# Window attention in a diffusion backbone: score products of full height, and the mask added where the row maximum is taken

## The chip, the cores and the metric

The kernel runs as one program on one core of a Trainium2 chip. The metric is the device time of one execution in microseconds (us), the median of several runs. The engines of the core work side by side, each through its own queue in order: TensorE (PE, with its weight loads shown apart as PEld), VectorE (DVE), ScalarE (ACT), GpSimd (POOL) and SyncE (SP), which issues most of the DMAs. Matrix products are summed in PSUM, and all other tiles lie in SBUF.

## What is computed

The reference is a stack of two layers over 256 latent tokens and 256 context tokens of width 1024. Each layer is a half-step SwiGLU FFN, a token mixer, and another half-step FFN; the mixer of layer 0 is a gated DeltaNet, that of layer 1 windowed attention with a sink per head. Only layer 1's mixer matters here, and only its latent queries, since the last layer's context output is not used:

```
s_ctx = einsum('bqhgd,bkhd->bhgqk', qb, kc)                 # 256 context keys, no mask
s_win = where(allowed, einsum('bqhgd,bkhd->bhgqk', qb, kb), -inf)   # |t - s| <= 128
p = _sink_softmax(concatenate([s_ctx, s_win]), sink)
o = einsum(p[..., :ctx_len], vc) + einsum(p[..., ctx_len:], vb)
```

There are 16 query heads of 64 features and 4 key heads; four query heads share one key head. With 256 latent tokens in two blocks of 128 queries, the window of a block covers all 256 latent keys, so every query sees 512 keys, and only one 128 by 128 corner of the latent keys is partly masked for each block.

## The kernel before

All products are made in a fast form of fp32 (`F32R`) that keeps the high part of a number alone. So each operand is split into a high part and a low part (number minus high part), and a product is made as high by high, high by low, and low by high, summed in PSUM. A weight matrix is loaded into a tile, split by ScalarE (high part) and by VectorE or GpSimd (low part) into working tiles, and then used.

The working tiles `u` are 76 buffers of 128 by 512 fp32 (256 KB each), and PSUM has 8 banks `mm`. The program is straight-line: the class `Sched` keeps an estimated clock of TensorE work and of each engine, and decides by it in which order the instructions are emitted. Background generators (`yield` gives the time at which they wish to be resumed) are woven between the products of the main line. On the chip nothing is reordered: each engine runs its instructions in the emitted order and waits for what they need.

The attention goes so:

- `att_consts` is started in the last part of the FFN ahead of it. It loads the constants over SP, among them the two triangles of the mask, and ScalarE copies these into `wmask`, 128 by 384: a triangle for either block with a zero square between, so that a slice of 256 columns is the mask of block 0 or block 1.
- `attention` makes keys and values first (four units of 128 columns for all 512 tokens), then the queries in 8 units of two heads, latent tokens only.
- `att_qk` norms and rotates a unit of two heads (64 rows each). For keys it writes the high part of each head twice, into rows 0 to 63 and 64 to 127 of a tile `st[par]`, and the low parts of both heads into one tile `lo`, each in its own 64 rows. For queries `st[par]` holds the high part in the head's own 64 rows and the low part in the other 64.
- Four `att_worker` generators take the 16 pairs of a query unit and a block. For each of the two heads of a pair (`par`), TensorE makes a score tile of 128 queries by 512 keys in three products: the query tile, 128 rows, with the doubled high keys (which gives high by high and low by high at once); the identity with the mask, 256 latent columns; and the high query, 64 rows, with the low keys, 64 rows. That is 32 score tiles in all. VectorE then takes the row maximum of each, ScalarE the exponential with the negative maximum as its bias and the row sum as a second output, VectorE scales by the reciprocal, TensorE transposes the probabilities, ScalarE copies them out, and TensorE multiplies them with the values.
- When few pairs are left, the output product begins (`begin`), and `out_blocks` finishes it and starts the next norm.

The score products and the maximum, as they stand (lines 1751 to 1760):

```
for par in range(2):
    rw = slice(64 * par, 64 * par + 64)
    sc.append(self.cht())
    self.mm(sc[par], q[par][:, qs], kh[par], stop=False)
    self.mm(sc[par][:, LAT], self.identr, self.wmask[:, 128 - 128 * qt:384 - 128 * qt], start=False, stop=False)
    self.mm(sc[par], q[par][rw, qs], kl[rw, :], start=False)
...
for par in range(2):
    nc.vector.tensor_reduce(out=st[:, 0, par:par + 1], in_=sc[par], axis=AX.X, op=ALU.max)
```

In the profile most instructions of VectorE, ScalarE, GpSimd and SP carry line 180, that of the helper that records them, products carry line 276 and transposes line 281, so groups are told apart by their tiles.

Of the kernel before, what the change touches and what calls it, by code (L numbers as in the profile page):

```python
# [6 lines left out]
F32R = mybir.dt.float32r  # L7
AF = mybir.ActivationFunctionType
ALU = mybir.AluOpType
# [13 lines left out]
def constants():  # L23
    """Arrays that depend on shapes alone."""
    c = {"ident": np.eye(128, dtype=np.float32)}
    # 128 rows: two chunks of 64 tokens; in variant e the half e runs forward and the other one backward
# [20 lines left out]
    d = np.arange(64)  # L47
# [13 lines left out]
    c["atc"] = at  # L61
    return c


class Sched:
    """Emission order: straight-line code advances a clock of TensorE work, and
    background generators are resumed when the clock reaches the time they asked for."""
# [9 lines left out]
    @staticmethod  # L77
    def cells(a):
        """a tile in parts of 64 partitions by 128 columns"""
        (ps, n), *rest = a.ap  # L80
        p, lo = divmod(a.offset, ps)
        hi = lo + sum((k - 1) * st for st, k in rest)
        return [(a.tensor.name, i, j) for i in range(p // 64, (p + n - 1) // 64 + 1)
                for j in range(lo // 128, hi // 128 + 1)]
# [8 lines left out]
    def note(self, eng, ins, outs, n, extra):  # L93
        """estimates when an instruction of another engine ends"""
# [14 lines left out]
    def product(self, ins, out, ns):  # L109
        """TensorE at the clock, other work first while the operands are awaited"""  # L110
# [59 lines left out]
class Queue:  # L170
    """an engine whose instructions are also noted in the schedule"""
# [38 lines left out]
class Kernel:  # L210
# [34 lines left out]
    def at(self, *aps):  # L245
        """time from now until these are expected"""
        return max(0.0, self.s.when(*aps) - self.s.clock)

# [35 lines left out]
    def mm3(self, ps, w, h, nk, sl=ALL, ks=None, start=True, stop=True):  # L284
        """ps[:, sl] = W^T h over nk chunks of 128, W and h in exact high and low parts."""
# [12 lines left out]
    def plan_weights(self):  # L298
        """Raw loads and the units of 128 output columns cut from them, in the order of use."""
# [4 lines left out]
        def raw(*parts):  # L304
            # outside of DeltaNet its tiles take loads as well
# [11 lines left out]
        def cols(mat, r0, nk, c0, w=256):  # L317
            """nk chunks of 128 rows from r0, w columns from c0 -> [128, nk, w]"""
# [91 lines left out]
    def _load(self, late=False):  # L410
        """loads into the raw tiles that are free, or soon (late = True: any that have no further use)"""
# [46 lines left out]
    def w_ahead(self):  # L458
        """splits the units to come once their loads are expected"""
# [29 lines left out]
    def setup(self):  # L489
# [18 lines left out]
        # tokens  # L508
# [6 lines left out]
        # modulation of the first norm and the first pairs of the first FFN, 128 features after the other  # L515
# [3 lines left out]
        # squares and transposes of the tokens  # L519
# [16 lines left out]
        # root mean squares of the tokens, from tokens on partitions to a row for every partition  # L536
# [12 lines left out]
    def setup_rows(self, rows):  # L549
        """vectors with their features on partitions"""  # L550
# [25 lines left out]
    def first_load(self, c):  # L576
        """weights of the first modulation and of the first pairs of the first FFN for 128 features"""
# [20 lines left out]
    def first_mod(self, c):  # L598
        """shift and scale of (layer 0, slot 0) for 128 features, and their norm"""
# [41 lines left out]
    def first_w(self, c):  # L641
        """high and low parts of the weights of 128 features"""
# [109 lines left out]
    def sq_block(self, d, sl, ps=None):  # L752
        """adds the squares of chunk d to the running sum"""
# [38 lines left out]
    def h_chunks(self, hf, l, slot, ks, pace=None):  # L792
        """high and low parts of the modulated norm of chunks ks, one group of tokens"""
# [70 lines left out]
    def mm_narrow(self, ps, w, sl):  # L864
        """W^T H for 32 columns in two parts: the high and the low part of W with the high part of H, and the high part
        and zeros with the low one"""
# [6 lines left out]
    def halves_first(self, n, evac, narrow=False):  # L873
        """the first n units, context tokens before latent ones"""
# [20 lines left out]
    def out_block(self, d, final):  # L895
        """the latent tokens of chunk d, tokens on partitions, to the output"""
# [15 lines left out]
    def out_blocks(self, h, nk, sl, l, v, nxt, final=None, begun=None):  # L912
        """X += gate * (W^T h); with nxt the squares of the sums and the next norm follow"""
# [77 lines left out]
    def start_pairs(self):  # L991
        """the first three pairs of the first FFN, chunk by chunk as the modulation arrives"""
# [19 lines left out]
    # Tokens of each segment are kept in the order of chunks 0, 3, 1, 2, so that 128 columns q hold the two chunks  # L1012
    # that the forward and the backward pass visit in the same step.
    # kinds of projection: 0 q, 1 k, 2 v, 3 z
# [38 lines left out]
    def dn_gates(self, ps):  # L1053
        """per-token gates from the projection in two parts of [32, 512], tokens on partitions, for both variants"""
# [58 lines left out]
    def dn_unit(self, kind, h, ps):  # L1113
        """evacuates the projection of head h: kind 0 q, 1 k, 2 v, 3 z"""
# [55 lines left out]
    def dn_ss(self, sq, g, dst):  # L1170
        """log of the sums of squares over the head dimension, tokens on partitions"""
# [14 lines left out]
    def dn_pairs(self, ps, lhs, rhs, g, qp):  # L1186
        """products over the head dimension inside each chunk, for two pairs of chunks and four heads"""
# [8 lines left out]
    def dn_prep(self, g):  # L1196
        """decays, the systems of each chunk and their inverses for the heads of group g"""
# [32 lines left out]
        # D[j, i] = exp(gc_i - gc_j) beta_j / (k_j.k_j + eps) where allowed, U = (k_j.k_i) D  # L1230
# [27 lines left out]
    def dn_decayed(self, g):  # L1258
        """keys times their decay to the end of the chunk, tokens on partitions"""
# [18 lines left out]
    def dn_solve(self, g):  # L1278
        """inverses of the unit triangular systems: 32 x 32 diagonal blocks by substitution, a block per partition,
        then the off-diagonal blocks of 64 x 64 on TensorE"""  # L1280
# [12 lines left out]
        # a block per partition: rows of the lower triangular system, transposed for the forward pass  # L1293
# [66 lines left out]
    def dn_kq(self, g):  # L1360
        """(k_j.q_i) D in place of D"""
# [21 lines left out]
    def dn_expand(self, g, k):  # L1383
        """for each step the inverses (k = 0) or the products of keys and queries of the four heads as block diagonals"""
# [138 lines left out]
    def dn_out(self, p):  # L1523
        """norm of o, gate and its high and low parts for a pair of heads"""
# [9 lines left out]
        # o is still to be scaled by the root of 1 / (q.q + eps) / 128  # L1534
# [35 lines left out]
    def begin(self, tasks, count, upto, sl=ALL):  # L1570
        """first part of the output product, as far as its operands are there"""
# [96 lines left out]
    def att_consts(self):  # L1668
# [5 lines left out]
        self.wmask = self.const([128, 384], "wmask", F32R)  # L1674
# [9 lines left out]
        for i, c0 in enumerate((384, 640, 256)):  # L1684
            if i == 1:
                self.act(out=self.wmask[:, 128:256], in_=t0[:, 256:384], func=AF.Copy, scale=0.0)
            else:
                self.act(out=self.wmask[:, 128 * i:128 * i + 128], in_=t0[:, c0:c0 + 128], func=AF.Copy)
        nc.vector.tensor_scalar(out=self.qg, in0=self.qg, scalar1=0.125, scalar2=None, op0=ALU.mult)

    def att_qk(self, ps, sl, gain, store, keys=False):
        """per-head norm and, for latent tokens, rotation of two heads"""
# [21 lines left out]
        # high parts of the two heads, twice for keys, and low parts: next to the high ones for queries  # L1714
        half = (slice(0, 64), slice(64, 128))
        st = [self.u(dt=F32R), self.u(dt=F32R)]
        lo = self.u(dt=F32R) if keys else None
        for par in range(2):
            for j in ((0, 1) if keys else (par,)):
                self.act(out=st[par][half[j], sl], in_=kn[half[par], sl], func=AF.Copy)  # L1720
        yield self.at(*st)
# [179 lines left out]
```

## Time and profile before

| What | Value |
|---|---|
| Median of 3 runs | 1941.55 us (1939.74 to 1942.11) |
| Profiled execution, span from first to last instruction | 1937.3 us |
| Mean granted TensorE clock | 0.991 |
| Instructions | 30131 |
| HBM traffic over the span | 258.34 MB read, 10.49 MB written |
| DMA packets' time, share of 16 engines | 42.4% (the main queue) |
| Keys, values and first queries, 1596 to 1624 us | ScalarE busy 24.91 of 28 us |
| The 32 score tiles, 1624 to 1703 us | TensorE busy 74.57 of 79 us |

The profile is of one execution of its own; the page gives its span, and the runs give whole times, which hold what lies ahead of the first and behind the last instruction as well. So the span stands 4.25 us below the median of the runs.

How to read the lines that follow: a group line gives the kernel's line, the engine and the operation, the tile written and the tiles read, the shape, the count, the busy time in us and the mean time of one in ns, and the idle time of the engine in front of these with what ended it. A timeline line gives start and duration in us, and in brackets the idle time before it. A stretch line gives start and end, the length, and the busy time and the count of each engine in the order that its head names, then the clock, the DMA share and GB/s. "128\*128" is rows by columns of the stationary operand of a product, and "64\*128" is one with 64 rows.

### The profile page before, as it was taken

What the parts mean: (1) busy time and instruction counts of PE and PEld (TensorE: products, weight loads), DVE (VectorE), ACT (ScalarE), POOL (GpSimd) and SP (SyncE); (2) the same over time, 40 slices, a digit from 0 to 9 for tenths busy, and PEclk for the clock granted to TensorE, in tenths of its full rate; (3) what the DMA queues carried; (4) which work ended last, traced back from release to release, by engine and by line L of the source; (5) the groups of instructions that cost most, each with busy time, mean ns of one, the idle gap of its engine ahead of it and who ended that gap; (6) DMA issues with size and microseconds to landing.
All of it is one profiled execution on the core that took longest, in us unless ns stands there. A gap on an engine that the chain in (4) does not pass through costs nothing.

```text
span 1937.3 us, 30131 instructions
## 1 busy us (share of the span) xinstructions
PE 1880.2 (97%) x11367; PEld 1560.9 (81%) x11367; DVE 1280.2 (66%) x2065; ACT 946.5 (49%) x2061; POOL 649.8 (34%) x597
## 2 busy tenths in 40 slices
PE   7999999989999999999999999999999999999999
PEld 5878788887776766887888888888888898689998
DVE  4897878855977966578888555643343356856565
ACT  4544544556476555464454344542222357755442
POOL 3344534454546435354445114320000057230000
PEclk8999999999999999999999999999999999999999
DMA  9655454413232152445645554433232334125552
GB/s 292 212 202 203 165 185 169 157 44 126 71 88 81 51 186 82 169 142 185 211 170 179 190 185 147 164 124 101 96 109 87 100 86 96 36 66 174 196 175 87
DMA packets 242376, 270.78 MB, mean 140 GB/s; under 512 B 11015, under 2 KB 198687, under 8 KB 242231
## 3 DMA queue, kind: packets, MB, share of 16 engines
q1 hardware_dynamic: 241943, 268.69, 42.4%
q8 instruction: 89, 1.46, 0.3%
q14 instruction: 56, 0.46, 0.1%
q0 software_dynamic: 144, 0.11, 0.0%
q10 hardware_dynamic: 144, 0.07, 0.0%
HBM read 258.34 MB, written 10.49 MB: 139 GB/s over the span
## 4 chain that ended last, share of the span: by engine, by line
PE 57%; DVE 6%; ACT 3%; issue 3%; POOL 1%; DMA 1%; POOLq 0%; DVEq 0%; ACTq 0%; SPq 0%
PE mm L276 56%; DVE u L180 5%; ACT u L180 3%; PE mm L281 1%; POOL u L180 1%; DVE st L180 1%; DVE big L180 0%; DMA u<-ZD 0%; DMA u<-XD 0%; DVE ub L180 0%; ACT L180 0%; POOLq L180 0%; DVEq L180 0%; ACT sc L180 0%; ACTq L180 0%
## 5 line engine op out<-in xcount | busy, mean ns | idle before, releaser
L276 PE MATMUL mm<-u 128*128 128x512 f32 (+6 forms) x10112 | 1798.5, 343 | 21.3 <-ACT u L180 9.6
L276 PEld LDWEIGHTS mm<-u 128*128 128x128 f32 (+2 forms) x10112 | 1491.4, 185 | 305.9 <-issue 54.4
L180 POOL TENSOR_TENSOR u<-u 128x512 f32<-128x512 f32 (+4 forms) x389 | 430.3, 1112 | 911.4 <-ACT u L180 868.3
L180 ACT ACTIVATE u<-u 128x256 f32<-128x256 f32 (+8 forms) x335 | 159.6, 488 | 488.1 <-DVE u L180 475.8
L180 ACT ACTIVATE u<-mm 128x512 f32<-128x512 f32 (+3 forms) x356 | 142.5, 414 | 283.1 <-PE mm L276 213.8
L180 DVE TENSOR_TENSOR u<-raw,u 128x512 fp32r<-128x512 f32 (+2 forms) x272 | 217.9, 845 | 27.3 <-ACT u L180 26.0
L180 DVE SCALAR_TENSOR_TENSOR u<-u,cc 128x512 f32<-128x512 f32 x196 | 229.3, 1170 | 3.9 <-DMA u<-in_ada_w 0.6
L180 DVE TENSOR_TENSOR u<-ub,u 128x512 fp32r<-128x512 f32 x254 | 199.8, 830 | 18.5 <-ACT u L180 17.3
L180 ACT ACTIVATE u<-raw 128x512 fp32r<-128x512 f32 (+1 forms) x374 | 205.8, 604 | 10.8 <-PE mm L276 5.7
L180 ACT ACTIVATE u<-u,cc 128x512 f32<-128x512 f32 x224 | 151.9, 711 | 82.5 <-DMA u<-in_ada_w 72.4
L180 DVE TENSOR_TENSOR u<-u,mm 128x512 f32<-128x512 f32 (+1 forms) x88 | 54.5, 619 | 206.5 <-PE mm L276 198.2
L180 POOL TENSOR_TENSOR u<-raw,u 128x512 fp32r<-128x512 f32 x98 | 130.4, 1354 | 135.7 <-ACT u L180 119.1
L180 ACT ACTIVATE u<-ub 128x512 fp32r<-128x512 f32 (+1 forms) x284 | 156.0, 605 | 10.2 <-DMA ub<-in_ffn_w 6.0
L180 DVE SCALAR_TENSOR_TENSOR u<-mm,mod,u 128x256 f32<-128x256 f32 x192 | 86.1, 478 | 106.4 <-PE mm L276 106.2
L180 DVE TENSOR_TENSOR u<-u 128x512 fp32r<-128x512 f32 (+5 forms) x125 | 82.6, 662 | 74.3 <-ACT u L180 72.5
L180 DVE SCALAR_TENSOR_TENSOR u<-u,mod 128x256 f32<-128x256 f32 (+1 forms) x140 | 88.8, 686 | 24.0 <-ACT u L180 23.7
L180 ACT ACTIVATE u<-u,mod 128x256 fp32r<-128x256 f32 (+1 forms) x124 | 56.2, 501 | 52.1 <-DVE u L180 51.7
L180 DVE SCALAR_TENSOR_TENSOR u<-mm,cw,u 128x510 f32<-128x510 f32 (+1 forms) x96 | 71.2, 743 | 8.1 <-ACT u L180 6.4
L281 PE MATMUL mm<-ident,u 128*128 128x128 f32 (+3 forms) x361 | 55.5, 283 | 11.3 <-DMA ident<-in_ident 4.4
L281 PEld LDWEIGHTS mm<-ident,u 128*128 128x128 f32 (+3 forms) x361 | 42.1, 145 | 23.5 <-ACT u L180 6.3
L276 PE MATMUL mm<-u,ones 128*32 128x512 f32 (+2 forms) x172 | 37.6, 551 | 14.5 <-DVE u L180 10.4
L180 POOL TENSOR_TENSOR u<-ub,u 128x512 fp32r<-128x512 f32 x30 | 41.5, 1406 | 22.1 <-ACT u L180 21.8
(118 smaller groups left out, 582.1 us busy)
## 6 DMA issues: line engine op xcount, KB each, us to landing
u<-in_ada_w SPq DMA_DIRECT2D x256, 256.0 KB, 5.6
ub<-in_ffn_w SPq DMA_DIRECT2D x59, 1024.0 KB, 5.1
raw<-in_ffn_w SPq DMA_DIRECT2D x57, 1024.0 KB, 5.1
raw<-in_dn_w_in SPq DMA_DIRECT2D x16, 1024.0 KB, 5.7
ub<-in_ada_w SPq DMA_DIRECT2D x12, 512.0 KB, 7.1
ub<-in_ffn_w SPq DMA_DIRECT2D x8, 768.0 KB, 4.6
raw<-in_ffn_w SPq DMA_DIRECT2D x8, 768.0 KB, 4.6
raw<-in_dn_w_out SPq DMA_DIRECT2D x4, 1024.0 KB, 6.2
```

What stands on the lines that cost most here:

```text
L180: r = f(*a, **k)
L276: self.nc.tensor.matmul(out, lhsT, rhs, start=start, stop=stop, **kw)
L281: self.nc.tensor.transpose(out, in_, self.ident[:k, :k])
```

## The change

It has three parts.

1. Low keys. `att_qk` writes the low part of each key head into a tile of its own, 128 rows high, whose other 64 rows ScalarE fills with zeros. The low product takes the whole query tile and that whole key tile.
2. Masks. The mask product is gone. The masks of the two blocks come ready from the host as an array of 128 by 1024 (`wmc`), zeros but for a triangle each, and are loaded into two working tiles that are held from then on. The three copies into the old `wmask` are gone.
3. Maximum. `tensor_tensor_reduce` on VectorE adds the mask to the score tile, writes the sum to the tile `P` in SBUF, and gives the row maximum as a second output. The exponential reads `P` and writes it in place, where it read PSUM before.

The diff without the lines that only remove comments:

```diff
@@ constants
+    wm = np.zeros((128, 1024), np.float32)
+    wm[:, 384:512] = at[:, 256:384]
+    wm[:, 768:896] = at[:, 384:512]
+    c["wmc"] = wm
@@ att_consts
-        self.wmask = self.const([128, 384], "wmask", F32R)
+        self.wmask = [self.u(), self.u()]
+        for i in range(2):
+            nc.sync.dma_start(out=self.wmask[i], in_=a["wmc"][:, 512 * i:512 * i + 512])
...
-        for i, c0 in enumerate((384, 640, 256)):
-            if i == 1:
-                self.act(out=self.wmask[:, 128:256], in_=t0[:, 256:384], func=AF.Copy, scale=0.0)
-            else:
-                self.act(out=self.wmask[:, 128 * i:128 * i + 128], in_=t0[:, c0:c0 + 128], func=AF.Copy)
@@ att_qk
-        lo = self.u(dt=F32R) if keys else None
+        lo = [self.u(dt=F32R), self.u(dt=F32R)] if keys else None
         for par in range(2):
             for j in ((0, 1) if keys else (par,)):
                 self.act(out=st[par][half[j], sl], in_=kn[half[par], sl], func=AF.Copy)
+            if keys:
+                self.act(out=lo[par][half[1 - par], sl], in_=kn[half[1 - par], sl], func=AF.Copy, scale=0.0)
...
-            dst = lo[half[par], sl] if keys else st[par][half[1 - par], sl]
+            dst = lo[par][half[par], sl] if keys else st[par][half[1 - par], sl]
@@ att_worker
-                rw = slice(64 * par, 64 * par + 64)
                 sc.append(self.cht())
                 self.mm(sc[par], q[par][:, qs], kh[par], stop=False)
-                self.mm(sc[par][:, LAT], self.identr, self.wmask[:, 128 - 128 * qt:384 - 128 * qt], start=False, stop=False)
-                self.mm(sc[par], q[par][rw, qs], kl[rw, :], start=False)
+                self.mm(sc[par], q[par][:, qs], kl[par], start=False)
...
             for par in range(2):
-                nc.vector.tensor_reduce(out=st[:, 0, par:par + 1], in_=sc[par], axis=AX.X, op=ALU.max)
+                P.append(self.u())
+                nc.vector.tensor_tensor_reduce(out=P[par], in0=sc[par], in1=self.wmask[qt], scale=1.0, scalar=NEG,
+                                               op0=ALU.add, op1=ALU.max, accum_out=st[:, 0, par:par + 1])
...
             for par in range(2):
-                P.append(self.u())
-                self.act(out=P[par], in_=sc[par], func=AF.Exp, bias=st[:, 1, par:par + 1],
+                self.act(out=P[par], in_=P[par], func=AF.Exp, bias=st[:, 1, par:par + 1],
                          accum_out=st[:, 2, par:par + 1])
```

The query tile holds the low part of the query in its other 64 rows; in the new low product these meet the zeros.

More of the change, by code (lines that the diff above doesn't have):

```diff
@@ L46, in constants @@
     at = np.zeros((128, 1024), np.float32)
-    d = np.arange(64)
     for b in (0, 64):
```

## The prediction

> **What bounds the kernel now.** I read the engine shares first, then the busy time by stretches, then the chain of waits and the TensorE lines of the stretch that the change touches. The shares (busy us, share of the span, instructions):
>
> ```profile
> PE 1880.2 (97%) x11367; PEld 1560.9 (81%) x11367; DVE 1280.2 (66%) x2065; ACT 946.5 (49%) x2061; POOL 649.8 (34%) x597
> ```
>
> TensorE is busy 97% of the span, but its ends are modelled, so this says only that it rarely stands idle, not that it works well. The attention is a small part of the span. Its stretches, each with the busy time of every engine:
>
> ```profile
> core 0 of [0], span 1937.3 us
> core 0: us, PE busy (x) PEld busy (x) DVE busy (x) ACT busy (x) POOL busy (x), PEclk, DMA share, GB/s
> 1596.00:1624.00 28.00, 27.29 (x202) 25.62 (x203) 10.37 (x15) 24.91 (x46) 23.12 (x21) 1.00 0.43 91
> 1624.00:1663.00 39.00, 37.08 (x253) 27.97 (x251) 32.84 (x70) 25.79 (x69) 19.97 (x21) 1.00 0.30 72
> 1663.00:1703.00 40.00, 37.49 (x274) 25.35 (x274) 31.32 (x90) 28.21 (x80) 2.85 (x3) 1.00 0.08 27
> ```
>
> The first row holds keys, values and the first queries. The next two, 79 us together, hold all score products (counted below). In these 79 us TensorE is busy 74.6 us (94%), VectorE 64.2 (81%), ScalarE 54.0 (68%). The clock is full, 1.00. The chain of waits inside the same 79 us, by line:
>
> ```profile
> by line: PE mm L276 56.0%; DVE st L180 14.0%; PE mm L281 13.3%; ACT u L180 8.4%; DVE u L180 7.3%; issue 1.0%; ACT st L180 0.2%
> ```
>
> So 69% of the chain is TensorE (56.0 + 13.3) and 21% VectorE (14.0 + 7.3): TensorE is the bound, with VectorE close behind. Now TensorE itself at the first score products (start, duration, form), and then its weight loads:
>
> ```profile
> 1624.50 0.28 PE L276 MATMUL mm<-wmask,identr 128*128 128x256 f32 x1
> 1624.71 0.92 PE L276 MATMUL mm<-u 64*128 64x512 f32 x2
> 1625.47 0.28 PE L276 MATMUL mm<-wmask,identr 128*128 128x256 f32 x1
> 1625.68 0.92 PE L276 MATMUL mm<-u 64*128 64x512 f32 x2
> ```
>
> ```profile
> 1624.71 0.18 PEld L276 LDWEIGHTS mm<-u 64*128 64x128 f32 x1 [0.25 <-issue]
> 1625.13 0.19 PEld L276 LDWEIGHTS mm<-u 128*128 128x128 f32 x1 [0.24 <-DVE u L180]
> 1625.24 0.19 PEld L276 LDWEIGHTS mm<-wmask,identr 128*128 128x128 f32 x1
> ```
>
> One score tile is high product, mask product, low product. From mask to mask it takes 1625.47 - 1624.50 = 0.97 us. The weight load of the 64-row low product stands 0.25 us before it starts, and so does the load after it (0.24), while the mask's load starts 0.11 us behind the one ahead of it, beside a running product. Over all tiles, and the tiles counted by the mask product in the two stretches (PE, PEld, ACT busy):
>
> ```profile
> L276 PEld LDWEIGHTS mm<-u 64*128 64x128 f32 x32 | 5.9, 183 | 7.9 <-issue 7.9
> 1624.00:1663.00 39.00, 3.90 (x14) 2.65 (x14) 0.00 (x0) 1.00 0.30 72
> 1663.00:1703.00 40.00, 5.01 (x18) 3.41 (x18) 0.00 (x0) 1.00 0.08 27
> ```
>
> 7.9 us of standing before 32 loads is 0.247 each: every low product pays it, 14 in the one stretch and 18 in the other. For a pace without changes of height I take a stretch of the FFN whose products are all 128 rows by 512 columns:
>
> ```profile
> 1480.00:1510.00 30.00, 30.00 (x134) 24.86 (x133) 10.68 (x17) 9.69 (x18) 0.00 (x0) 1.00 0.31 105
> ```
>
> 30.0 / 134 = 0.224 us a product.
>
> **TensorE's part of the change.** A tile becomes two full-height products of 512 columns, 2 x 0.224 = 0.448 us, against 0.97 now: 0.52 us less, of which the mask product is 0.112 (256 columns, half of 0.224) and the two changes of height with the loads that they expose the rest. Times 32 this is 16.7 us of TensorE time, 7.3 in the first stretch and 9.4 in the second. TensorE's demand falls from 74.6 to 57.9 us of 79. It is not what the time falls by: VectorE is next, with 64.2 us before anything is added to it.
>
> **VectorE's part.** 32 row maxima over PSUM become 32 instructions that read PSUM and a mask in SBUF, write the sum to SBUF and keep the maximum. The rows (min/median/max ns) of the old form and of the exponential behind it, two maxima in a row, ScalarE's accumulator read with the activation after it, and the nearest VectorE row with a PSUM and an SBUF source:
>
> ```profile
> L180 DVE TENSOR_REDUCE st<-mm x32: 675/681/692, 1625.3 to 1701.7; 128x1 f32<-128x512 f32 x32
> L180 ACT ACTIVATE u<-mm,st x32: 669/687/722, 1629.6 to 1706.3; 128x512 f32<-128x512 f32 x32
> L180 ACT ACTIVATION_READ_ACCUMULATOR u<-mm,st x32: 187/206/243, 1630.2 to 1706.9; 128x1 f32 x32
> ```
>
> ```profile
> 1670.66 1.28 DVE L180 TENSOR_REDUCE st<-mm 128x1 f32<-128x512 f32 x2
> ```
>
> ```profile
> 1630.19 0.19 ACT L180 ACTIVATION_READ_ACCUMULATOR u<-mm,st 128x1 f32 x1
> 1630.28 0.68 ACT L180 ACTIVATE u<-mm,st 128x512 f32<-128x512 f32 x1
> ```
>
> ```profile
> L180 DVE SCALAR_TENSOR_TENSOR u<-mm,cw,u 128x508 f32<-128x508 f32 x48 | 35.7, 744 | 1.2
> ```
>
> Two maxima take 1.28 us, so the second adds 1.28 - 0.68 = 0.60. The trace before has no such fused instruction. Lower bound of its extra: nothing, if it runs at the pace of the maximum; I see no reason for a gain, as it streams the same 512 columns. Upper bound: the two-source row's 0.744 - 0.681 = 0.06, and a separate accumulator read as long as ScalarE's, 0.21: 0.27. I take 0.12: half of the 0.06, and 0.09 for the read, which is how far ScalarE's next start lies behind its read (1630.28 - 1630.19). Times 32: 3.8 us, bounds 0 and 8.6. VectorE's demand becomes 68.0 us (64.2 to 72.8).
>
> [...]
>
> **ScalarE's part.** The exponential reads SBUF instead of PSUM. Both sources at 512 columns, then the stretch where the keys are prepared, and the TensorE group behind it:
>
> ```profile
> 1600.63 0.63 ACT L180 ACTIVATE u<-u 128x512 f32<-128x512 f32 x1
> 1601.17 0.58 ACT L180 ACTIVATE u<-mm 128x512 f32<-128x512 f32 x1
> ...
> 1606.98 2.55 ACT L180 ACTIVATE u<-u 64x512 fp32r<-64x512 f32 x4
> ...
> 1611.72 2.55 ACT L180 ACTIVATE u<-u 64x512 fp32r<-64x512 f32 x4
> 1614.30 0.38 ACT L180 ACTIVATE u<-mm 128x256 f32<-128x256 f32 x1
> ```
>
> ```profile
> 1614.73 9.93 PE L276 MATMUL mm<-u 128*128 128x256 f32 x70 [0.28 <-ACT u L180]
> ```
>
> 0.05 us more for each of 32 exponentials is 1.6 us, hidden while ScalarE has 25 us free in the 79; without that cover it would be 1.6. The zero halves add four 64x512 activations, two behind each group of four copies: 2.55 / 4 x 4 = 2.5 us. ScalarE is busy 24.9 of 28 us there. Queued behind the added ones are the weight copies and the square at 1614.30, and TensorE starts at 1614.73 after waiting for ScalarE. So between 0 and 2.5 us come on the path; other products can go ahead if their weights are split, POOL being busy 23.1 of 28, so not for long. I take 1. The three mask copies that go were far earlier.
>
> **The rest, at nothing.** Two more 256 KB loads go to SP's queue with the constants:
>
> ```profile
> 1526.31 1.00 SPq L180 DMA_DIRECT2D u<-in_atc  x2
> ...
> 1529.16 1.23 SPq L180 DMA_DIRECT2D kg<-in_swa_k_gain  x2
> 1536.73 0.39 SPq L180 DMA_DIRECT2D raw<-in_swa_w_qkv  x1
> ```
>
> Two issues take 1.0 us. They pass the small constants, and the next weight load comes 6 us after the last of those (1529.16 + 1.23 to 1536.73), so that gap hides them; without it, 1 us. Two working tiles of 76 are held to the end and one more per pair of keys, which could let a weight split wait; I see no row that prices it, and put it between 0 and 1 us, at 0. Score banks come free after the maximum, not after the exponential: TensorE stands 4.4 us of the 79 (79 - 74.6), which bounds that gain; I count 0.
>
> **The sum.** Two estimates of the new length of the 79 us. If VectorE, now the bound, gets the share that the bound has today: 68.0 / 0.944 = 72.0, a gain of 7.0. If the three engines' shares add up as today, (74.6 + 64.2 + 54.0) / 79 = 2.44, then (57.9 + 68.0 + 55.6) / 2.44 = 74.4, a gain of 4.6. I take 6, less 1 in the key stretch: 5 us. The span goes from 1937.3 to 1932.3. The median of the runs, 1941.55, lies 4.25 above the span; I leave that difference as it is: **1936.5 us**. The rest of the span only moves forward.
>
> **The rivals.**
> *All of TensorE's saving shows*: the fused instruction costs no more than the maximum and VectorE packs better when fed sooner. 64.2 / 0.944 = 68.0 gives 11 - 1 = 10 us; the whole 16.7 - 1 = 15.7. So 1926 to 1932. For it: TensorE has 69% of the chain. Against: VectorE would have to be busy over 94% of 68 us.
> *The gain is eaten*: VectorE at its upper bound, 72.8 / 0.944 = 77.1, a gain of 1.9, and the key stretch costs 2.5: 1942. For it: ScalarE is on the chain up to 1614.73. From 1938 to 1944.
> *Slower*: the fused instruction makes two passes over its 512 columns, so 2 x 0.60 = 1.20 us. VectorE's demand is then 64.2 + 32 x 0.60 = 83.4, or 88.3 us at 94.4%: 9.3 longer, and 1 for the keys: 1952. It decides from an extra of (0.944 x 79 - 64.2) / 32 = 0.32 us a tile, 0.92 us in all. Against it: the two-source row, 744 ns for 508 columns, and the row with both sources in SBUF,
>
> ```profile
> L180 DVE SCALAR_TENSOR_TENSOR u<-u,cc x196: 736/752/1869, 56.3 to 1254.5; 128x512 f32<-128x512 f32 x196
> ```
>
> whose median is 752. [...]
> *The stall is not the height's*: then only the mask's 32 x 0.112 = 3.6 us leave TensorE, (74.6 - 3.6) / 0.944 = 75.2 at best, and with VectorE's and ScalarE's additions the time stays, 1939 to 1942. Against it: the 0.247 us stands before every 64-row load and before no mask load.
>
> **How the numbers follow.** Forecast, 1933.5 to 1938.5: 0.42. All shows: 0.22. Eaten: 0.20. Slower: 0.10. Not the height: 0.06. A measurement of this kernel tells about 0.2% from no change, 3.9 us. Faster by more: all of the second case and 0.37 of the forecast, 0.59. Within: 0.05 + 0.20 + 0.06 = 0.31. Slower: 0.10. The range, 1927 to 1943, leaves out the slower case and the ends of two others.
>
> **What would show it.** Right: tiles 0.45 us apart where two follow each other; no standing before low loads; VectorE over 90% busy between the first and the last tile; the fused instruction spaced 0.65 to 0.8 us. Wrong: a spacing over 0.92, TensorE's wait near the keys above 2 us, or VectorE still near 80% with the time unchanged, which would mean that the order of emission, not an engine, holds it.

## The result, and the profile after

| | before | after |
|---|---|---|
| median of 4 runs each | 1941.83 us (1939.74 to 1942.39) | 1930.90 us (1928.68 to 1932.89) |
| ratio, 95% interval | 1 | 0.9941 [0.9929, 0.9953] |
| span of the profiled execution | 1937.3 us | 1926.9 us |
| attention stage (see below) | 146.74 us | 136.09 us |

The kernel became 10.9 us faster by the medians and 10.4 us by the profiled spans. That is inside the range and on the side of the forecast, but a little over twice the gain of the likeliest case, 5 us: it lies in the first rival, "All of TensorE's saving shows".

The page of the changed kernel, engine shares (busy us, share of the span, instructions):

```profile
PE 1868.2 (97%) x11335; PEld 1558.2 (81%) x11335; DVE 1278.8 (66%) x2097; ACT 949.4 (49%) x2062; POOL 649.3 (34%) x597
```

TensorE has 12.0 us less than before (1880.2) and 32 products less. VectorE has 32 instructions more and yet 1.4 us less (1280.2 before). So the fused maxima, with whatever was added to them, cost VectorE nothing that its total shows.

The median of the kernel before is 1941.83 us here, 1939.03 on the chip of the first group of experiments and 1940.91 on those of the other two, so I measure the attention by itself, from a table load of ScalarE as the attention begins to the first one behind it. (One more load stands between, 3.03 us behind the former in both kernels.) The timelines of ScalarE, first before, then after:

```profile
1595.59 1.28 ACT L180 ACT_TABLE_LOAD   x1
...
1742.33 1.28 ACT L180 ACT_TABLE_LOAD   x1
```

```profile
1596.03 1.28 ACT L184 ACT_TABLE_LOAD   x1
...
1732.12 1.28 ACT L184 ACT_TABLE_LOAD   x1
```

1742.33 - 1595.59 = 146.74 us, and 1732.12 - 1596.03 = 136.09 us after: 10.65 us less, which is all of the gain. The **stage**, start to start of these two loads, is the measure for the experiments as well. The changed kernel profiled once more gave 136.07, in this one repeat far closer than whole times are to each other.

The stretches of the changed kernel (columns as before: length, then busy time of PE, PEld, DVE, ACT, POOL, the clock, DMA share, GB/s):

```profile
1596.00:1624.00 28.00, 27.25 (x203) 25.34 (x203) 9.39 (x12) 26.75 (x50) 20.21 (x18) 1.00 0.39 76
...
1624.00:1694.00 70.00, 61.67 (x508) 50.63 (x507) 64.65 (x193) 56.39 (x154) 25.63 (x27) 1.00 0.24 61
1631.00:1694.00 63.00, 54.95 (x466) 44.81 (x465) 60.26 (x187) 51.54 (x143) 18.79 (x20) 1.00 0.19 51
1671.00:1689.00 18.00, 18.00 (x163) 14.45 (x165) 17.16 (x67) 15.82 (x45) 0.00 (x0) 1.00 0.00 1
```

From the first maximum (1631.08) to the last (1693.06) VectorE is busy 60.26 of 63 us, 96%. In the last row, the steady part, TensorE shows no idle time at all and VectorE is busy 17.16 of 18. The chain of waits from 1624 to 1692, by line:

```profile
by line: DVE u L184 46.3%; PE mm L280 25.9%; DVE st L184 10.9%; PE mm L285 10.8%; issue 6.4%
```

VectorE has gone from 21% of the chain to 57%, TensorE from 69% to 37%. VectorE's timeline in the steady part, for one pair of tiles:

```profile
1677.46 0.68 DVE L184 CUSTOM_DVE_ANT_0 u<-mm,u 128x512 f32<-128x512 f32 x1
1678.06 0.08 DVE L184 DVE_READ_ACCUMULATOR2_ANT st<- 128x1 f32 x1
1678.06 0.69 DVE L184 CUSTOM_DVE_ANT_0 u<-mm,u 128x512 f32<-128x512 f32 x1
1678.67 0.08 DVE L184 DVE_READ_ACCUMULATOR2_ANT st<- 128x1 f32 x1
1678.79 0.16 DVE L184 SCALAR_TENSOR_TENSOR st<-st,nsink 128x2 f32<-128x2 f32 x1
...
1680.45 0.68 DVE L184 CUSTOM_DVE_ANT_0 u<-mm,u 128x512 f32<-128x512 f32 x1
```

`CUSTOM_DVE_ANT_0` is the fused maximum. The second starts 1678.06 - 1677.46 = 0.60 us behind the first, as two plain maxima did, and its accumulator read of 0.08 us is a row of its own that starts together with the next maximum. From one pair to the next it is 1680.45 - 1677.46 = 2.99 us. TensorE's timeline over the same pairs, eight transposes and then twenty products (four for the scores, sixteen for the values):

```profile
1677.00 1.09 PE L285 MATMUL mm<-ident,u 128*128 128x128 f32 x8
1677.85 2.19 PE L280 MATMUL mm<-u 128*128 128x512 f32 x20
1680.00 1.12 PE L285 MATMUL mm<-ident,u 128*128 128x128 f32 x8
```

3.00 us a pair, without idle time. So in the steady part both engines are taken up for about 3.0 us a pair. That TensorE has no room to spare there is shown by e6b below, since a busy TensorE alone does not show it.

### The profile page after: what moved, and what is told of

Read it like the earlier page. It is cut to its first block, busy times and chain, and to the rows that moved or that the text cites. A ratio compares the mean times of both kernels' runs of the same rounds, so it can differ in the third digit from the quotient of the medians.

```text
span 1926.9 us, 30122 instructions
## 1 busy us (share of the span) xinstructions
PE 1868.2 (97%) x11335; PEld 1558.2 (81%) x11335; DVE 1278.8 (66%) x2097; ACT 949.4 (49%) x2062; POOL 649.3 (34%) x597
## 4 chain that ended last, share of the span: by engine, by line
PE 55%; DVE 7%; ACT 3%; issue 3%; POOL 1%; DMA 1%; POOLq 0%; DVEq 0%; ACTq 0%; SPq 0%
PE mm L280 54%; DVE u L184 7%; ACT u L184 3%; PE mm L285 1%; POOL u L184 1%; DVE st L184 0%; DVE big L184 0%; DMA u<-ZD 0%; DMA u<-XD 0%; DVE ub L184 0%; ACT L184 0%; POOLq L184 0%; DVEq L184 0%; DVE sc L184 0%; ACT sc L184 0%
## 5 line engine op out<-in xcount | busy, mean ns | idle before, releaser
L280 PE MATMUL mm<-u 128*128 128x512 f32 (+5 forms) x10112 | 1784.9, 342 | 21.2 <-ACT u L184 8.2
L184 ACT ACTIVATE u<-u 128x512 fp32r<-128x512 f32 (+8 forms) x339 | 162.1, 490 | 494.0 <-DVE u L184 478.7
L184 ACT ACTIVATE u<-mm 128x128 f32<-128x128 f32 (+3 forms) x356 | 141.7, 413 | 262.4 <-PE mm L280 199.4
```

Of the source, the lines that this page charges most:

```text
L184: r = f(*a, **k)
L280: self.nc.tensor.matmul(out, lhsT, rhs, start=start, stop=stop, **kw)
```

## The experiments

Two names run through the expectations. A is the leading theory of a run, in most of them that the time that left is TensorE's, above all that of the change of height, and that VectorE bounds the tiles now. B is the rival that the run is to tell from it. A pair is two score tiles; its period is read from one row of eight transposes to the next. The first group of four, the second (e4 to e7) and the third (e8 to e10) were run on a chip each, with the kernel before beside them. The medians and ratios are of several executions, but each stage is read from one profiled execution.

| Run | stage us | median us | ratio to before, 95% |
|---|---|---|---|
| changed kernel again | 136.07 | 1930.31 | 0.9950 [0.9937, 0.9964] |
| e1 height only | 139.03 | 1931.89 | 0.9954 [0.9940, 0.9969] |
| e2 mask only | 139.91 | 1932.80 | 0.9959 [0.9945, 0.9974] |
| e3 zeros early | 134.40 | 1928.26 | 0.9937 [0.9923, 0.9950] |
| e4 fused maximum twice | 154.54 | 1948.05 | 1.0035 [1.0023, 1.0046] |
| e5 plain maximum twice, before | 157.19 | 1950.00 | 1.0043 [1.0026, 1.0060] |
| e6 high product twice | 140.66 | 1932.79 | 0.9954 [0.9940, 0.9969] |
| e7 half of the scaling on GpSimd | 134.53 | 1930.50 | 0.9941 [0.9928, 0.9954] |
| e8 order only | 144.27 | 1938.05 | 0.9986 [0.9976, 0.9995] |
| e9 banks held | 140.48 | 1933.53 | 0.9966 [0.9953, 0.9979] |
| e6b high product twice, same order | 137.89 | 1930.76 | 0.9951 [0.9936, 0.9966] |
| e10 five workers | 135.79 | 1928.71 | 0.9937 [0.9922, 0.9952] |

**The changed kernel again**, as the measure of how well the stage repeats.

> The changed kernel unaltered, on the chip of the following three, as their yardstick. Both theories: about 10.9 us below the kernel before, 1931 us.

136.07 against 136.09 us for the stage. The whole time is 8.7 us below the kernel before by the medians, with an interval that reaches from 7.0 to 12.2 and holds the 10.9. I read differences of half a microsecond between stages as real, on this one repeat.

The profiled executions differ in one thing that the stages hide, TensorE's granted clock. Read in steps of 1 us, ahead of the last 30 us of the stage, it is 1.00 throughout in both kernels, the repeat, e2, e8 and e10. In the others it falls to 0.50 for a while: for some 3.4 us in e3, e6b and e7, 6.8 in e1, e5 and e6, 10.2 in e9 and 17 in e4. Where that bears on a reading it is said.

**e1, the height alone.** The kernel before with two padded low keys; mask product and plain maximum stay.

```diff
+                self.act(out=lo[par][half[1 - par], sl], in_=kn[half[1 - par], sl], func=AF.Copy, scale=0.0)
...
-                self.mm(sc[par], q[par][rw, qs], kl[rw, :], start=False)
+                self.mm(sc[par], q[par][:, qs], kl[par], start=False)
```

> Only the low keys are padded to full height; the mask product and the plain row maximum stay. Theory A (the height costs TensorE 0.41 us a tile, and VectorE is the next bound): TensorE saves 13 us, VectorE's 64.2 us are unchanged, so 8 to 10 us faster than before, 1932 to 1934, nearly all of the change's gain; no standing before low loads. Theory B (the gain comes from the mask product's removal, and from score banks that come free after the maximum): 0 to 3 us slower than before, since only the zero halves on ScalarE are added.

The stage is 7.7 us shorter, and by the medians the whole is 7.1: A, a little short of its 8. The order of the instructions moved here too (see e8) and the clock fell later on, so the spacing of the tiles, read at full clock, is the surer reading. TensorE's timeline where tiles follow each other:

```profile
1634.99 0.28 PE L276 MATMUL mm<-wmask,identr 128*128 128x256 f32 x1
1635.11 0.62 PE L276 MATMUL mm<-u 128*128 128x512 f32 x2
1635.57 0.28 PE L276 MATMUL mm<-wmask,identr 128*128 128x256 f32 x1
```

From mask to mask 0.58 us in place of 0.97: the height is worth 0.39 us a tile here, and the forecast had 0.41 (0.52 less the mask's 0.112).

**e2, the mask alone.** The changed kernel with the low keys back in one tile and a 64-row low product.

```diff
-                self.mm(sc[par], q[par][:, qs], kl[par], start=False)
+                self.mm(sc[par], q[par][rw, qs], kl[rw, :], start=False)
```

> Only the masks move to VectorE; the low product stays 64 rows high and is still led by a load that stands. Theory A: TensorE saves 32 x 0.112 = 3.6 us, less where the load now stands behind the high product as well; 0 to 3 us faster than before, 1939 to 1942. Theory B: 7 to 11 us faster, 1931 to 1935.

The stage is 6.8 us shorter, so A's 0 to 3 did not hold, and B's 7 to 11 was nearly reached. The mask's own 32 x 0.112 = 3.6 us can't give this. The weight loads show that the change of height is still paid for in full:

```profile
1624.85 0.18 PEld L280 LDWEIGHTS mm<-u 64*128 64x128 f32 x1 [0.24 <-issue]
1625.27 0.19 PEld L280 LDWEIGHTS mm<-u 128*128 128x128 f32 x1 [0.24 <-DVE u L184]
1625.70 0.18 PEld L280 LDWEIGHTS mm<-u 64*128 64x128 f32 x1 [0.24 <-issue]
```

So something else had changed in e2 too. Each kernel's instructions are emitted in an order that the scheduler works out from its estimates, and those include the mask product and the maximum. e8 was made to test this.

**e8, the order alone.** The kernel before, doing all of its own work; the scheduler alone takes the mask product for 0 ns and the maximum for 65 ns longer.

```diff
-                self.mm(sc[par][:, LAT], self.identr, self.wmask[...], start=False, stop=False)
+                self.mm(sc[par][:, LAT], self.identr, self.wmask[...], start=False, stop=False, ns=0.0)
...
-                extra = len(outs) - 1 + ...
+                extra = (n == "tensor_reduce" and size == 512) + len(outs) - 1 + ...
```

> The kernel before, instruction for instruction, but emitted in the order of the kernel with the masks alone on VectorE: the planner counts the mask product at 0 ns and the maximum with 65 ns more. The masks alone had shortened the stretch between ScalarE's table loads around the attention from 146.7 to 139.9 us, 6.8 us, where the mask product's 3.6 us of TensorE was expected. Theory A (the new order is worth the rest): 143 to 144 us here, 3 us faster than before. Theory B (the rest comes from score banks that come free after the maximum): 146 to 148 us here, no gain.

144.27 us, 2.5 less than before and close to A's 143 to 144: the order alone gives 2.5 us. In the traces of e8, e2 and e3 every engine now runs in the same order, but for the instructions that the edits themselves change. So the three differ only by these instructions, and the stage can be taken apart step by step:

| Step | stage, us | difference |
|---|---|---|
| before to e8: order of emission | 146.74 to 144.27 | -2.5 |
| e8 to e2: mask to VectorE, score banks free earlier, exponential from SBUF, masks loaded ready | 144.27 to 139.91 | -4.4 |
| e2 to e3: full height (zeros written early) | 139.91 to 134.40 | -5.5 |
| e3 to the changed kernel: zeros between the keys, and the order that follows | 134.40 to 136.09 | +1.7 |

Of these kernels only e3 has a stretch of lower clock, and VectorE is busy 4.70 of the 5 us from 1661 to 1666 that hold it, so it can have cost little. The steps are those of this sequence; another one might share the time out otherwise.

The transposes tell the mask and the height apart in the steady part. The pair of e8:

```profile
1677.26 1.09 PE L281 MATMUL mm<-ident,u 128*128 128x128 f32 x8
...
1681.05 1.09 PE L281 MATMUL mm<-ident,u 128*128 128x128 f32 x8
```

of e2:

```profile
1673.74 1.09 PE L285 MATMUL mm<-ident,u 128*128 128x128 f32 x8
...
1677.31 1.09 PE L285 MATMUL mm<-ident,u 128*128 128x128 f32 x8
```

and of e3:

```profile
1679.69 1.09 PE L285 MATMUL mm<-ident,u 128*128 128x128 f32 x8
...
1682.68 1.09 PE L285 MATMUL mm<-ident,u 128*128 128x128 f32 x8
```

3.79, 3.57 and 2.99 us: 0.22 a pair for the mask, which is its 2 x 0.112, and 0.58 a pair for the height, 0.29 a tile and not 0.41. The weight loads of e2 and e3 in these pairs point to the reason. e2 (score loads, then the first value load, 64 columns wide):

```profile
1674.99 0.18 PEld L280 LDWEIGHTS mm<-u 64*128 64x128 f32 x1 [0.24 <-issue]
1675.42 0.19 PEld L280 LDWEIGHTS mm<-u 128*128 128x128 f32 x1 [0.25 <-issue]
1675.85 0.18 PEld L280 LDWEIGHTS mm<-u 64*128 64x128 f32 x1 [0.24 <-issue]
1676.28 0.85 PEld L280 LDWEIGHTS mm<-u 128*64 128x64 f32 x16 [0.24 <-ACT u L184]
```

e3:

```profile
1677.54 0.77 PEld L280 LDWEIGHTS mm<-u 128*128 128x128 f32 x4
1678.67 0.85 PEld L280 LDWEIGHTS mm<-u 128*64 128x64 f32 x16 [0.36 <-ACT u L184]
```

Four loads go back to back in e3, but the load of the values behind them stands 0.36 us (0.24 in e2). So of a pair's four changes of height the last falls on a place where a load stands anyway. Three of four times 0.41 is 0.31 a tile, near the 0.29. This is argued from the rows; no run tries it alone.

**e3, the zeros early.** The changed kernel with the zero halves written with the constants, ahead of the attention.

```diff
+        self.klo = [[self.u(dt=F32R), self.u(dt=F32R)] for _ in range(2)]
+        for lo in self.klo:
+            for par in range(2):
+                self.act(out=lo[par][half[1 - par], :], in_=t0[half[1 - par], :], func=AF.Copy, scale=0.0)
...
-        lo = [self.u(dt=F32R), self.u(dt=F32R)] if keys else None
+        lo = self.klo.pop(0) if keys else None
...
-            if keys:
-                self.act(out=lo[par][half[1 - par], sl], in_=kn[half[1 - par], sl], func=AF.Copy, scale=0.0)
```

> The changed kernel with the four zero halves written in the FFN ahead, where ScalarE has time, not between the copies of the keys. Theory A (the zero halves delay the keys on ScalarE and part of it stays on the path): 1 to 2.5 us faster than the changed kernel, first score tile some 3 us sooner. Theory B (the delay is filled with query products pulled ahead and costs nothing): within 0.7 us of it.

1.7 us shorter than the changed kernel, as A had it, and the shortest stage of the study. The whole time is 1928.26 us beside 1930.31 on the same chip, with intervals that overlap. The first maximum starts 29.70 us into the stage, in the changed kernel 35.05: 5.35 us sooner, where A had some 3. ScalarE's timeline of the changed kernel has the keys' copies and zeros together:

```profile
1607.49 3.85 ACT L184 ACTIVATE u<-u 64x512 fp32r<-64x512 f32 x6
...
1613.24 3.86 ACT L184 ACTIVATE u<-u 64x512 fp32r<-64x512 f32 x6
```

Six take 3.85 where four took 2.55, twice 1.3 = 2.6 us, of which 1.7 show. The order differs between the two as well, so 1.7 is both together.

**e4, the fused maximum twice.** In the changed kernel each is issued a second time into a spare column.

```diff
+                nc.vector.tensor_tensor_reduce(out=P[par], in0=sc[par], in1=self.wmask[qt], scale=1.0, scalar=NEG,
+                                               op0=ALU.add, op1=ALU.max, accum_out=st[:, 6, par:par + 1])
```

> The changed kernel with every fused maximum issued twice (the second result is not used): 32 x 0.61 = 19.5 us more of VectorE in the score stretch. Theory A (VectorE is the bound there, busy 27.6 of 29 us): 15 to 19 us slower than the changed kernel. Theory B (the order of emission or another engine holds the stretch): under 10 us slower.

The stage is 18.45 us longer for 32 x 0.61 = 19.5 us of VectorE: 95% is paid, A. The stretch in the middle:

```profile
1672.00:1700.00 28.00, 22.51 (x170) 16.81 (x171) 26.81 (x92) 17.25 (x48) 0.00 (x0) 0.88 0.01 1
```

VectorE is busy 26.81 of 28, TensorE 22.51: with more of it VectorE is the one bound. That holds beside the lower clock too. In the 67 us that contain its 17 us at 0.50 VectorE stands no more than 2.7 us in all:

```profile
1645.00:1712.00 67.00, 52.67 (x390) 40.10 (x388) 64.28 (x215) 44.73 (x123) 5.72 (x7) 0.87 0.05 17
```

**e5, the plain maximum twice**, in the kernel before: the same test at the old bound.

```diff
+                nc.vector.tensor_reduce(out=st[:, 6, par:par + 1], in_=sc[par], axis=AX.X, op=ALU.max)
```

> The kernel before with every row maximum issued twice (the second result is not used): 32 x 0.60 = 19.2 us more of VectorE. Theory A (TensorE is the bound before, VectorE has some 15 us free in the 79): 6 to 12 us slower than before, clearly less than the added work. Theory B (VectorE was the bound already): 15 to 19 us slower.

10.45 us longer for 32 x 0.60 = 19.2 us, A: 54% paid. Before, VectorE had room for nearly half of it, or for more, since e5 holds 6.8 us at a clock of 0.50 that the kernel before does not have. In e4 and e5 the scheduler knew of the added instructions, and TensorE's order changed with them. An order was worth 2.5 us in e8, which would be 13% of what was added: too little to close the gap between 54% and 95%.

**e6, the high product twice** in the changed kernel, TensorE's counterpart of e4.

```diff
+                self.mm(sc[par], q[par][:, qs], kh[par])
                 self.mm(sc[par], q[par][:, qs], kh[par], stop=False)
```

> The changed kernel with every high score product made twice (the first sum is dropped by the start of the second): 32 x 0.224 = 7.2 us more of TensorE. Theory A (VectorE is the bound after the change): 0 to 3 us slower than the changed kernel. Theory B (TensorE is still the bound): 6 to 7 us slower.

4.6 us longer for 32 x 0.224 = 7.2 us, between A and B. The scheduler knew of the product and made another order, so e6b repeats it from e3 with the product kept from the scheduler. (e6 also holds 6.8 us at a clock of 0.50, where the changed kernel has none.)

```diff
+                nc.nc.tensor.matmul(sc[par], q[par][:, qs], kh[par], start=True, stop=True)
                 self.mm(sc[par], q[par][:, qs], kh[par], stop=False)
```

> The changed kernel with early zeros, in the same order of emission, with every high score product made twice without the planner's knowledge: 7.2 us more of TensorE. In the changed kernel's own order of planning the same addition cost 4.6 us of the stretch. Theory A (VectorE alone is the bound): under 1.5 us longer than 134.4. Theory B (TensorE and VectorE are about equally loaded, so either's extra is paid): 4 to 7 us longer.

3.5 of 7.2 us: half, and again neither of the two. Here the order is that of e3, and so is the time at the lower clock, 3.4 us. TensorE's timeline of e6b in the steady part:

```profile
1676.50 1.09 PE L285 MATMUL mm<-ident,u 128*128 128x128 f32 x8
...
1679.93 1.09 PE L285 MATMUL mm<-ident,u 128*128 128x128 f32 x8
```

3.43 us a pair, 0.44 more than in e3, which is the two added products in full (2 x 0.224). VectorE shows an idle time now that it did not have:

```profile
1678.32 0.69 DVE L184 CUSTOM_DVE_ANT_0 u<-mm,u 128x512 f32<-128x512 f32 x1 [0.26 <-PE mm L280]
```

So in the steady part TensorE is the bound as soon as it gets more; elsewhere most of the added products are hidden.

**e7, half of the scaling on GpSimd**, from e3, to see whether a relieved VectorE shortens the stage.

```diff
-                nc.vector.tensor_scalar(out=P[par], ...)
+                (nc.gpsimd if par else nc.vector).tensor_scalar(out=P[par], ...)
```

> The changed kernel with early zero halves, and the scaling of every second probability tile on GpSimd instead of VectorE: 16 x 0.5 = 8 us less of VectorE, GpSimd being idle from 1663 to 1692 us but busy with weight parts before. Theory A (VectorE is the bound): 2 to 6 us faster than the kernel with early zeros alone. Theory B: no faster, or slower by GpSimd's longer instruction in the chain of a pair.

134.53 us, the same as e3's 134.40: B's "no faster", and not A's 2 to 6 us. The groups by tile:

```profile
L184 DVE TENSOR_SCALAR u<-u,st x16: 485/487/1280, 1638.4 to 1700.4; 128x512 f32<-128x512 f32 x16
...
L184 POOL TENSOR_SCALAR u<-u,st x16: 1559/1762/1853, 1639.4 to 1701.0; 128x512 f32<-128x512 f32 x16
```

VectorE lost 16 of 32, but GpSimd needs 1.76 us for what took 0.49, and in some places the loads of the transposes wait for it, 0.8 us in all from 1670 to 1700. Where two pairs follow each other without such a wait, their first loads are 1680.74 - 1677.76 = 2.98 us apart, as the pairs of e3 are. That speaks for TensorE as what holds e7, but the order changed as well, and the run does not part these.

**e9, the banks held.** From e3; behind each exponential ScalarE reads one column of the score tile, so the bank comes free as late as before. The added output is used nowhere.

```diff
+                nc.nc.scalar.activation(out=st[:, 7, par:par + 1], in_=sc[par][:, 0:1], func=AF.Copy)
```

> The changed kernel with early zeros, in the same order of emission, but ScalarE also reads one element of the score tile behind each exponential, so that its bank is held as long as before. Theory A (the banks do not matter): 134.4 us between the table loads plus up to 1.5 us for 32 short instructions of ScalarE. Theory B (they do): 2 to 4 us or more longer.

6.1 us longer than e3, so B, which said 2 to 4 or more. By the medians, each against the kernel before on its own chip, it is 3.4 us longer. All but 0.1 of it is there before the steady part: the first of its transposes starts 78.98 us into the stage, in e3 72.98. TensorE's timeline:

```profile
1637.41 0.70 PE L280 MATMUL mm<-u 128*128 128x256 f32 x2 [0.75 <-ACT st L1774]
...
1643.51 8.24 PE L280 MATMUL mm<-u 128*128 128x256 f32 x50 [3.15 <-DVE u L184]
```

The first row is a product that waits for the added read (line 1774) to give up its bank; the second waits for VectorE. The added instructions also take ScalarE's time, though little of it, by the starts on its timeline:

```profile
1679.46 0.20 ACT L184 ACTIVATION_READ_ACCUMULATOR u<-u,st 128x1 f32 x1
1679.55 0.17 ACT L1774 ACTIVATE st<-mm 128x1 f32<-128x1 f32 x1
1679.61 0.73 ACT L184 ACTIVATE u<-u,st 128x512 f32<-128x512 f32 x1
```

0.06 us a tile, 1.9 us in all. The other 4 us are not the waits alone, since the clock falls behind them. First e9, then e3 at the same place of the stage:

```profile
1641.00:1648.00 7.00, 4.49 (x17) 4.14 (x18) 4.14 (x9) 3.77 (x13) 2.75 (x2) 0.55 0.39 126
```

```profile
1637.00:1644.00 7.00, 6.28 (x56) 5.55 (x55) 6.72 (x13) 6.92 (x21) 5.19 (x6) 1.00 0.49 152
```

The granted clock is 0.55 in place of 1.00, TensorE shows 17 products in place of 56, and VectorE stands 2.9 us of the 7. So holding the banks cost time as a whole. How much of it is the waits and how much is the slower clock behind them isn't separated.

**e10, five workers** in place of four, from e3 (`range(5)`), to see whether more pairs in flight fill the early part.

> The changed kernel with early zeros and five score generators instead of four. Theory A (engines are the bound): within 1 us of 134.4 us between the table loads. Theory B (the latency of a pair's chain holds four generators): 1 to 4 us shorter.

1.4 us longer than e3, outside what both theories said, with a ratio to before that can't be told from e3's. The order changes with the number of workers, and I draw nothing more from it.

## Why the forecast was right, and its size not

**The bound and its successor: right.** TensorE was the bound, and e1 and the step from e2 to e3 show that the change of height is the largest part of what it paid; VectorE came next. e4 and e5 show the move: added VectorE time was paid at 54% before, at 95% after. What the forecast did not have is that TensorE ends at the same 3.0 us a pair (e6b).

**TensorE's part: right where tiles follow each other, too large in the steady part.** 0.39 of the forecast 0.41 us for the height in e1's early tiles, but 0.29 in the pairs, probably since the values' loads stand there anyway.

**VectorE's part: the term that was too large.** The prediction took 0.12 us extra a tile, 3.8 us in all, with bounds 0 and 0.27. From a pair's first maximum to the operation behind the two, VectorE's rows of after (shown above) have 1678.79 - 1677.46 = 1.33 us. Before, the two maxima that start at 1670.66 are followed by this row of VectorE's timeline:

```profile
1671.97 0.16 DVE L180 SCALAR_TENSOR_TENSOR st<-st,nsink 128x2 f32<-128x2 f32 x1
```

1671.97 - 1670.66 = 1.31 us. So the extra is 0.02 us a pair, 0.3 us over the 16 pairs: the lower bound was nearly true. Neither part of the 0.12 showed: not the 0.03 from the row with two sources, and not ScalarE's 0.09 between its accumulator read and its next start, taken as the price of VectorE's read. The trace after does have 32 accumulator reads beside the 32 maxima. What did not hold is my estimate of 0.09 us a tile for it:

```profile
L184 DVE DVE_READ_ACCUMULATOR2_ANT st<- x32: 77/83/85, 1631.7 to 1693.7; 128x1 f32 x32
```

Each lasts 0.083 us, and the first of a pair lies beside the start of the second maximum (1678.06 in the rows above).

**The sum: a value between two estimates, of which the first was nearer.** With the measured extra, VectorE's demand is 64.2 + 0.3 = 64.5 us, and the first estimate gives 64.5 / 0.944 = 68.3, a gain of 10.7. It takes VectorE to be busy 94.4%; over the stretch from 1624 to 1694 that was 64.65 / 70 = 92%. The second held that the three engines' shares add up to 2.44 as before. They add up to (61.67 + 64.65 + 56.39) / 70 = 2.61 in the same stretch: the engines overlap better than before. I had taken a value between the two, 6.

**The keys: right in kind, low in size.** 1 us was taken on the path; 1.7 us was measured (e3), together with the order that follows, inside the bounds 0 and 2.5.

**What was not priced: the order.** The scheduler's estimates changed with the instructions, and that gave 2.5 us (e8). With it the corrected sum is 10.7 - 1.7 + 2.5 = 11.5 us, and 10.65 was measured. That the unpriced order more than made up for the keys is luck, and that the sums nearly agree is a check and no proof; the table of steps under e8 is measured directly.

**The edits at nothing.** The exponential from SBUF takes 0.711 us in place of 0.687, 0.024 more where 0.05 was taken. It was counted as hidden, which no run tries alone. Its row in the changed kernel:

```profile
L184 ACT ACTIVATE u<-u,st x32: 705/711/725, 1635.8 to 1696.2; 128x512 f32<-128x512 f32 x32
```

Banks that come free earlier were counted at 0. In e2, with TensorE still slow, mask, banks and exponential together gave 4.4 us, of which the mask's TensorE time is 3.6. If that is paid in full, the banks were worth at most about 0.8 there. With the faster TensorE of e3 giving them up later cost more, some 4 us of the stage (e9), a fall of the clock included. So they look less like a gain of their own than like a condition of the gain, which is argued and not shown. The two added loads and the tiles held longer were not tried by themselves.

**The rivals.** "All shows" came nearest, and by its own condition: the fused instruction costs no more than the maximum, and VectorE is busy 96% between the first maximum and the last, over the 94% that I doubted. The order's 2.5 us were not in that case either; without them, by the table of steps, the gain would be some 8 us, between it and the forecast. "Slower" needed a spacing over 0.92 us; it is 0.60, below the 0.65 to 0.8 of the forecast. "Eaten" needed 0.27 extra. "The stall is not the height's" falls with e1's spacing and with the step from e2 to e3.

## What to carry to other kernels

Where an added instruction isn't in the trace, look at what it overlaps on its own engine before taking another engine's spacing as its price; here the lower bound was right. When the bound is lifted, ask for each part of the loop which engine comes next: double a suspected instruction on each engine and see what share is paid, since a balanced loop can charge for both. Here VectorE's was paid at 95% (e4) and TensorE's at half (e6b), while less work for VectorE gained nothing (e7, 134.53 us beside 134.40). Read the granted clock of each stretch beside it: in e9 it fell to 0.50 behind and beside a wait of 3.15 us that came with the edit, and then the price may not be the edit's alone. In a kernel whose order is planned from estimates, every edit moves the order too: separate it by giving the old kernel the new estimates.

## What the runs showed of the hardware that was not expected

- Adding a mask from SBUF in the instruction that takes the maximum costs VectorE 0.60 us of spacing for 128 by 512, as the plain maximum does.
- A change from 128-column to 64-column weights stands too: 0.36 us ahead of the load in e3. Its row names ScalarE as the releaser, but in e6b, where the pair is longer, the same load stands as long with no releaser, which speaks for the shape; it was not tried alone. TensorE's weight loads of e6b:

```profile
1682.34 0.85 PEld L280 LDWEIGHTS mm<-u 128*64 128x64 f32 x16 [0.36 <-issue]
```

- The same scaling of a 128 by 512 tile takes GpSimd 1.76 us and VectorE 0.49.
- TensorE's granted clock can fall in the middle of a kernel. In e9 it is 0.50 from 1642 to 1648 us, behind and beside a wait of 3.15 us. In e4's middle stretch, where TensorE has 22.51 busy us of 28, it is 0.88, while it is 1.00 in the full stretch of the changed kernel. No run shows what sets the clock, and TensorE's busy share over a long stretch does not tell it alone. In the changed kernel TensorE is busy less, 11.33 of 16 us, and keeps its full clock:

```profile
1640.00:1656.00 16.00, 11.33 (x85) 8.98 (x85) 15.40 (x38) 12.44 (x33) 7.66 (x8) 1.00 0.39 126
```
